# Value projection, first column pass: the fourth and the seventh chunk as seven block products

## The chip, the cores and the metric

The kernel runs on one core of a Trainium2 chip. The metric is the device time of one execution in microseconds (us), the median of three runs: 1117.72 us, from 1116.6 to 1118.2. A profile of one execution stands beside it.

## The reference, cut to what matters

The reference is one decoder layer on 256 tokens of width 2048, in float32: a combined projection, two groups of eight attention heads, an output projection, a layer norm, a gated feed-forward block with a short convolution, and a second layer norm. The change touches only the value columns of the first projection:

```python
proj = h @ w_in[l]            # h: 256 x 2048
v_d = proj[..., o0:o0 + DIFF_W]   # 8 heads x 128 columns
v_m = proj[..., o0:o0 + MOBA_W]   # 8 heads x 128 columns
```

Together that is a product of a 256 x 2048 matrix with a 2048 x 2048 matrix.

## The kernel before, in words

**Precision.** Each float32 operand is split into two fp32r parts, hi (a rounded copy, written by ScalarE, ACT) and lo (the rest, a subtraction by VectorE, DVE). A product of two operands is three matmuls: hi by hi, hi by lo, lo by hi. In the value projection the activations (tile x2, read as xh and xl) are the stationary side and 512 weight columns the moving side.

**Tiling.** The value projection runs in two column passes of 1024 columns. A pass goes over the 2048 rows of the weights in eight chunks of 256. Chunks are numbered 0 to 15 in the order of the list `stream`: 0 to 7 are the first pass, 8 to 15 the second. The fourth and the seventh chunk of the first pass are chunks 3 and 6. The four sums of a pass, two token halves by two column halves, stay in PSUM banks 0 to 3 (CB). A plain chunk is 2 x 2 x 2 blocks, eight products of three matmuls each: 24 matmuls of 128x512 (`mm_pair`).

**Seven products.** In chunks 9, 12 and 15 the eight products are replaced by seven (Winograd's form): the weights and the activations of a chunk are first combined into block sums, and of the seven products four (numbers 1, 5, 6 and 7) are shared by several of the four results. They gather in banks 4 to 7 (MB) and are added up once, at the end of the pass (`v_shared`). That is 21 matmuls (`mm_seven`), issued in the order 5, 7, 6, 4, 1, 2, 3. Products 5, 7, 6 and 4 read weight sums in the slots 3, 4, 5 and 6 of the tiles vhi and vlo, and products 1, 2 and 3 read the plain weight blocks in the slots 0 to 2. The lo part of slots 0 to 2 isn't made by DVE: ACT writes the negated hi part, and a DMA issued on POOL adds the raw weights to it (L626 and L627). vhi and vlo have one buffer each, so a second such chunk can't be prepared before TensorE is done with the one before it.

**Order of work.** Nothing is scheduled by a planner: each engine runs its instructions in the order in which the code is written. `begin(i)` comes before chunk i and prepares chunk i + 2, `middle(i)` stands in it, and a list of due steps (`at`, `pending`, `urgent`) adds what has to be done at a given chunk. For a chunk of seven products `begin(i)` calls `blocks_raw` and `act_sums` for chunk i + 2, `middle(i)` calls `blocks_lo`, `blocks_sum`, `act_sums_split`, `blocks_hi` and the split of chunk i + 3, and `begin(i + 1)` finishes slot 6. The engines ACT and DVE run ahead of TensorE as far as their inputs and their buffers allow. Raw weights come through the queue of SP into four slots in turn (raw0 to raw3), so chunk 7 reuses the slot of chunk 3, and chunk 10 that of chunk 6.

The lines the text speaks of: L177 and L179 make hi and lo of a plain chunk, L228 and L229 hi and lo of the activations, L626 to L633 are `blocks_raw`, L638, L655 and L661 the lo, the sum and the hi of the slots 3 to 6, L586 to L589 and L604 and L605 the sums of the activations and their split, L861 the copy of a finished bank, L855 and L858 `v_shared`, and L277 every matmul.

Of the kernel before, what the change touches and what calls it, by code (L numbers as in the profile page):

```python
# [11 lines left out]
F32 = mybir.dt.float32  # L12
F32R = mybir.dt.float32r
AF = mybir.ActivationFunctionType
ALU = mybir.AluOpType

P = 128
# [25 lines left out]
PT = FT // 2  # L43
VP = KT // 2


SEVEN = {"v": ((), range(1, 8, 3)), "d": (range(PT - 2), range(3, 16, 3))}

LATE = 2

# [7 lines left out]
def hymba_layer(ctx: ExitStack, tc: tile.TileContext, a: dict):  # L58
    nc = tc.nc
    PE, DVE, ACT, POOL, SP = nc.tensor, nc.vector, nc.scalar, nc.gpsimd, nc.sync  # L60

    def pool(name, bufs=1, space=None):
        kw = {} if space is None else {"space": space}
        return ctx.enter_context(tc.tile_pool(name=name, bufs=bufs, **kw))
# [3 lines left out]
    work = pool("work", 2)  # L68
# [157 lines left out]
    def split_x(k0, k1):  # L226
        t = xraw[:, k0 * S:k1 * S].rearrange("p (k t) -> p k t", t=S)
        ACT.activation(xh[:, k0:k1], t, AF.Copy)  # L228
        DVE.tensor_tensor(xl[:, k0:k1], t, xh[:, k0:k1].bitcast(F32), ALU.subtract)  # L229
# [83 lines left out]
    vals = keep.tile([P, 4, 2, 512], F32, name="val", tag="big")  # L313
# [5 lines left out]
    def at(step, fn, *args, rank=LATER):  # L319
        after.setdefault(step, []).append((rank, len(after.get(step, ())), fn, args))  # L320
# [205 lines left out]
    def down_slot():  # L526

        if "slot" not in kept:
            kept["slot"] = keep.tile([P, 16, 512], F32R, name="slot", tag="t2")
        return kept["slot"]  # L530
# [22 lines left out]
    aparts, sums = {}, {}  # L553
    sevens = [p for kind, p, n, j in stream if (kind, n) == ("d", 1) and j in SEVEN["d"][1]]

    def seven(i):
        kind, p, n, j = stream[i]
        return kind in SEVEN and (j if kind == "d" else p) in SEVEN[kind][n] and (kind, n) != ("d", 0)

# [52 lines left out]
    def blocks_raw(i):  # L612

        kind, p, n, _ = stream[i]
        t = loaded[i].rearrange("p (b c) -> p b c", c=512)
        if kind == "d":
            slot = down_slot()
            hi, lo = slot[:, 0:7], slot[:, 7:14]
        else:
            lo = keep.tile([P, 7, 512], F32R, name="vlo", tag="ma")  # L620
            hi = keep.tile([P, 7, 512], F32R, name="vhi", tag="mb")
        b11, _, b22, b12 = ORDER[kind]
        f = [work.tile([P, 512], F32, name="tf", tag="m1") for _ in range(2)]
        blocks[i] = (hi, lo, f)
        if kind == "v":
            ACT.activation(lo[:, 0:3], t[:, 0:3], AF.Copy, scale=-1.0)  # L626
            POOL.dma_start(lo[:, 0:3], t[:, 0:3], accum_op=ALU.add)  # L627
        DVE.tensor_tensor(f[0], t[:, b11], t[:, b12], ALU.subtract)
        DVE.tensor_tensor(f[1], t[:, b12], t[:, b22], ALU.add)
        for j in range(2):  # L630
            ACT.activation(hi[:, 3 + j], f[j], AF.Copy)
        if kind == "v":
            ACT.activation(hi[:, 0:3], t[:, 0:3], AF.Copy)  # L633
# [31 lines left out]
    MB = {1: bank[4], 5: bank[5], 6: bank[6], 7: bank[7]}  # L665
# [22 lines left out]
    def mm_pair(i, c, k):  # L688

        kind, _, n, _ = stream[i]  # L690
        ah, al = aparts[i, k]
        w = weights(i, 1024 * c + 512 * k, 512)
        for lhs, j in ((ah, 0), (al, 0), (ah, 1)):
            for t in range(2):
                mm_count((kind, n, t, c), CB[t][c], lhs[:, t * P:(t + 1) * P], w[j])

    def mm_seven(i, then={}):
        kind, _, n, _ = stream[i]
        hi, lo, _ = blocks.pop(i)
        s3, s1, s2, s4 = sums.pop(i)  # L700
        (h0, l0), (h1, l1) = (aparts[i, k] for k in ((0, 1) if kind == "d" else (1, 0)))
        a11, a12, a22 = (h0[:, 0:P], l0[:, 0:P]), (h1[:, 0:P], l1[:, 0:P]), (h1[:, P:], l1[:, P:])
        b11, b21, b22, _ = ORDER[kind]
        for m, lhs, b in ((5, s1, 3), (7, s3, 4), (6, s2, 5), (4, a22, 6), (1, a11, b11), (2, a12, b21), (3, s4, b22)):
            t, c = {2: (0, 0), 3: (0, 1), 4: (1, 0)}.get(m, (None, None))
            key, dst = ((kind, n, m), MB[m]) if t is None else ((kind, n, t, c), CB[t][c])
            if m == 4:
                middle(i)
            mm_three(key, dst, lhs, (hi[:, b], lo[:, b]))
            if m in then:  # L710
                then[m]()
# [62 lines left out]
    for kind, pairs in (("v", VP), ("d", PT)):  # L774
        for n in range(2):
            np_ = pairs - (PAIRED_END if kind == "d" and n == 1 else 0)
            n7 = len(SEVEN[kind][n])
            for m in MB:
# [20 lines left out]
    def begin(i):  # L799

        urgent(i)
        j = i + 2
        if j < NS and seven(j):
            blocks_raw(j)
            act_sums(j)
        elif j - 1 < NS and seven(j - 1):
            blocks_sum(j - 1, 1)
            split(j, 1)
            blocks_hi(j - 1, 1)
            blocks_lo(j - 1, 3)  # L810
            blocks_whole(j - 1)
        else:
            split(j, 0)
            split(j, 1)
        if i >= first_d:
            act_back(i + 3)
        load(i + 6)
        pending(i)

    def middle(i):  # L820

        urgent(i + 0.5)
        if i + 2 < NS and seven(i + 2):
            blocks_lo(i + 2, 0)
            blocks_sum(i + 2, 0)
            blocks_lo(i + 2, 1)
            act_sums_split(i + 2)
            blocks_hi(i + 2, 0)
            split(i + 3, 0)
            blocks_lo(i + 2, 2)  # L830
        elif i + 3 < NS and not seven(i + 3):
            split(i + 3, 0)
        pending(i + 0.5)
# [10 lines left out]
    def done(i):  # L844
        for half in range(2):
            parts.pop((i, half))

    def value(n, t, c):
        return vals[:, 2 * n + c, t]

    def v_shared(n):
# [4 lines left out]
        for t, c, m in ((0, 1, 5), (1, 1, 5), (0, 0, 0), (None, None, 6), (0, 1, 0), (None, None, 7), (1, 0, 0), (1, 1, 0)):  # L856
            dst = u if t is None else v[t, c]
            DVE.tensor_tensor(dst, dst, MB[m] if m else u, ALU.add)  # L858

    def v_copy(n, t, c):  # L860
        ACT.activation(value(n, t, c), CB[t][c], AF.Copy)  # L861

    def run_v(i):
        _, p, n, _ = stream[i]
        for k in range(2):
            aparts[i, k] = xh[:, 2 * p + k], xl[:, 2 * p + k]
        if i == first_q - 1:
            v_copy(1, 1, 1)
            mm_seven(i, {m: lambda tc=tc: v_copy(1, *tc) for m, tc in ((2, (0, 0)), (3, (0, 1)), (4, (1, 0)))})
            at(i + 1, v_shared, 1)  # L870
        elif seven(i):
            mm_seven(i)
        elif i < 2:
            for k in range(2):
                if k == 1:
                    middle(i)
                for c in range(2):
                    mm_pair(i, c, k)
            done(i)
        else:  # L880
            for c in range(2):
                if c == 1:
                    if i == VP - 1:
                        for t in range(2):
                            v_copy(0, t, 0)
                    middle(i)
                for k in range(2):
                    mm_pair(i, c, k)
            done(i)
        if i == VP - 1:  # L890
            for t in range(2):
                at(i + 1, v_copy, 0, t, 1, rank=0)
        for k in range(2):
            aparts.pop((i, k))

# [27 lines left out]
    for i in range(first_o):  # L923
        begin(i)
        if i < first_q:
            run_v(i)
        else:
            run_a(i)
        if i == 8:
            load_consts()  # L930
        if i == 11:
            lambdas()
        if i == 14:
            SP.dma_start(z, a["x"])
        if i == 14:
            load_table("cos_m")
            load_table("sin_m")
# [17 lines left out]
    for i in range(first_o, last[0]):  # L955
# [11 lines left out]
        if first_o + 8 <= i < first_o + 12:  # L967
            n = i - first_o - 8
# [326 lines left out]
    for i in range(first_d, NS - PAIRED_END):  # L1295
        begin(i)
        _, p, n, j = stream[i]
# [203 lines left out]
```

## Time and profile before

| | |
|---|---|
| median of 3 runs | 1117.72 us |
| lowest and highest run | 1116.6 and 1118.2 us |
| span of the profiled execution, first to last instruction | 1115.1 us |
| what the median has beyond that span | 2.6 us |
| PE busy in the span | 1105.6 us (99%) |
| DVE and ACT busy | 853.6 us (77%) and 682.1 us (61%) |
| first pass of the value projection on PE | from 4.69 to 49.67 us |

Of the profiled execution only the span is known, so its own time is taken as the span and 2.6 us around it. PE is TensorE's matmuls. In rows of the timeline the first number is the start in us from the beginning of the span, the second the us from the start of the first to the end of the last instruction in the row, then the engine, the line, the operation with its tiles and shapes, how many there are, and in brackets how long the engine had been idle and what ended that.

### The profile page before, as it was taken

The numbers are of one execution on the slowest core, as the hardware profiler recorded it, in microseconds if no ns is written. First come the engines' busy times: TensorE is split into PE (matmuls) and PEld (weight loads), VectorE is DVE, ScalarE is ACT, GpSimd is POOL, SyncE is SP. The second block draws the span as 40 slices with busy tenths as digits, with TensorE's granted clock in tenths as the row PEclk, the third lists the DMA queues.
The fourth block names the chain that finished last, engine by engine and source line by source line (L and its number), as shares of the span: only waits on it lengthen the run. The fifth ranks groups of instructions, "written<-read, shape, count | busy, mean of one in ns | idle before, by whom it ended". The sixth has DMA issues, their size and how long they took to land.

```text
span 1115.1 us, 15769 instructions
## 1 busy us (share of the span) xinstructions
PE 1105.6 (99%) x5929; PEld 952.2 (85%) x5929; DVE 853.6 (77%) x1400; ACT 682.1 (61%) x1077; POOL 57.4 (5%) x81
## 2 busy tenths in 40 slices
PE   9999999999999999999999999999999999999997
PEld 6888888888888898888888888888888888888886
DVE  6676778887745778878888887777777777678866
ACT  6655776644443486666666666666666666645552
POOL 0000110000000000000000000000000000001103
PEclk9999999999999999999999999999999999999999
DMA  9898866444455537977877877777777777688992
GB/s 330 281 285 288 258 199 199 165 152 157 174 198 189 189 116 260 295 255 246 268 258 258 267 247 250 255 238 259 248 247 249 244 245 252 199 320 296 324 323 77
DMA packets 59868, 266.46 MB, mean 239 GB/s; under 512 B 6080, under 2 KB 7568, under 8 KB 42000
## 3 DMA queue, kind: packets, MB, share of 16 engines
q1 hardware_dynamic: 51584, 229.81, 57.1%
q0 software_dynamic: 8064, 35.39, 14.2%
q8 instruction: 46, 0.75, 0.3%
q10 hardware_dynamic: 144, 0.26, 0.1%
q14 instruction: 30, 0.25, 0.1%
HBM read 227.93 MB, written 15.20 MB: 218 GB/s over the span
## 4 chain that ended last, share of the span: by engine, by line
PE 98%; DVE 1%; DMA 0%; ACT 0%; issue 0%; SPq 0%; DVEq 0%
PE bank L277 97%; PE bank L404 0%; DMA raw<-in_w_v 0%; PE bank L987 0%; PE bank L451 0%; ACT hf L990 0%; DVE h L1002 0%; DVE st L475 0%; DVE z L472 0%; DVE z L1349 0%; DVE z L1345 0%; DVEq L1497 0%; DVE mv L481 0%; ACT hi L208 0%; DVE h L1001 0%
## 5 line engine op out<-in xcount | busy, mean ns | idle before, releaser
L277 PE MATMUL bank<-h,hi 128*128 128x512 f32 x1376 | 480.9, 390 | 0.0
L277 PE MATMUL bank<-h,lo 128*128 128x256 f32 x1376 | 387.9, 282 | 0.0
L277 PEld LDWEIGHTS bank<-h,hi 128*128 128x128 f32 x1376 | 258.2, 188 | 54.5
L277 PEld LDWEIGHTS bank<-h,lo 128*128 128x128 f32 x1376 | 260.0, 189 | 3.7
L179 DVE TENSOR_TENSOR lo<-raw,hi 128x1024 fp32r<-128x1024 f32 x147 | 177.1, 1221 | 92.3 <-ACT hi L177 91.6
L196 DVE TENSOR_TENSOR lo<-raw,hi 128x1024 fp32r<-128x1024 f32 x171 | 206.8, 1220 | 25.1 <-ACT hi L188 24.9
L177 ACT ACTIVATE hi<-raw 128x1024 fp32r<-128x1024 f32 x155 | 161.5, 1055 | 86.4 <-PE bank L277 55.9
L277 PE MATMUL bank<-x,hi 128*128 128x512 f32 x512 | 183.4, 399 | 0.0
L188 ACT ACTIVATE hi<-raw 128x1024 fp32r<-128x1024 f32 x171 | 177.3, 1050 | 0.0
L277 PE MATMUL bank<-x,lo 128*128 128x256 f32 x512 | 144.3, 282 | 0.0
L1107 ACT ACTIVATE ub<-bank 128x512 f32<-128x512 f32 x86 | 51.4, 598 | 108.2 <-PE bank L277 105.2
L277 PEld LDWEIGHTS bank<-x,hi 128*128 128x128 f32 x512 | 96.2, 188 | 21.9 <-issue 2.7
L277 PEld LDWEIGHTS bank<-x,lo 128*128 128x128 f32 x512 | 96.8, 189 | 0.2
L1116 DVE TENSOR_TENSOR ub<-ub 128x256 f32<-128x256 f32 x86 | 36.4, 423 | 56.9 <-ACT ub L1107 56.9
L742 ACT ACTIVATE tslot<-tf 128x512 fp32r<-128x512 f32 x80 | 50.3, 628 | 43.5 <-DVE tf L1197 24.7
L745 DVE TENSOR_TENSOR tslot<-tf,tslot 128x512 fp32r<-128x512 f32 x80 | 55.2, 690 | 12.4 <-ACT tslot L742 10.3
L277 PE MATMUL bank<-hi,back 128*128 128x512 f32 (+1 forms) x216 | 58.9, 381 | 0.0
L277 PE MATMUL bank<-hi,x 128*128 128x512 f32 x208 | 56.0, 391 | 0.8 <-ACT hi L208 0.8
L277 PE MATMUL bank<-tslot,sp 128*128 128x512 f32 x180 | 47.8, 392 | 0.0
L277 PEld LDWEIGHTS bank<-hi,x 128*128 128x128 f32 x208 | 38.8, 188 | 9.9 <-ACT hi L208 2.0
L277 PEld LDWEIGHTS bank<-hi,back 128*128 128x128 f32 x216 | 40.2, 188 | 7.8
L277 PE MATMUL bank<-hi,mh 128*128 128x512 f32 x128 | 41.2, 394 | 0.0
(233 smaller groups left out, 1460.6 us busy)
## 6 DMA issues: line engine op xcount, KB each, us to landing
raw<-in_w_u SPq DMA_DIRECT2D x88, 1024.0 KB, 6.2
raw<-in_w_d SPq DMA_DIRECT2D x68, 512.0 KB, 6.8
raw<-in_w_qk SPq DMA_DIRECT2D x32, 1024.0 KB, 4.9
raw<-in_w_o SPq DMA_DIRECT2D x16, 1024.0 KB, 4.8
raw<-in_w_v SPq DMA_DIRECT2D x28, 512.0 KB, 7.6
ring<-in_w_d SPq DMA_DIRECT2D x20, 512.0 KB, 7.1
dparts<-rslot SPq DMA_DIRECT2D x20, 512.0 KB, 2.8
back<-dparts POOLq DMA_DIRECT2D x19, 512.0 KB, 7.2
```

Source lines behind the costliest of these rows:

```text
L177: ACT.activation(hi[:, s], t[:, x:y], AF.Copy)
L179: DVE.tensor_tensor(lo[:, s], t[:, x:y], hi[:, s].bitcast(F32), ALU.subtract)
L188: ACT.activation(hi, t[:, half * 1024:half * 1024 + 1024], AF.Copy)
L196: DVE.tensor_tensor(lo, t[:, half * 1024:half * 1024 + 1024], hi.bitcast(F32), ALU.subtract)
L277: PE.matmul(out, lhsT, rhs, start=start, stop=stop)
L742: ACT.activation(side["t"][:, 0, j], f, AF.Copy)
L745: DVE.tensor_tensor(side["t"][:, 1, j], f, side["t"][:, 0, j].bitcast(F32), ALU.subtract)
L1107: ACT.activation(t.rearrange("p j t -> p (j t)"), up_bank(i), AF.Copy)
L1116: DVE.tensor_tensor(u[:, 0], u[:, 0], u[:, 1], ALU.add)
```

## The change

The table SEVEN gets chunks 3 and 6 of the first pass. The block sums for them are made in the same way, at the same places of `begin` and `middle`; `blocks_raw` also splits the activations of its chunk, which the plain split did before. The shared products of chunks 3 and 6 are added up by `v_products` in the middle of chunk 7, into the part of the tile `vals` that belongs to the second pass and is still empty, and `v_sum` adds that part to the first pass's values in the middle of chunk 9.

```diff
-SEVEN = {"v": ((), range(1, 8, 3)), "d": (range(PT - 2), range(3, 16, 3))}
+SEVEN = {"v": (range(3, 8, 3), range(1, 8, 3)), "d": (range(PT - 2), range(3, 16, 3))}
...
             hi = keep.tile([P, 7, 512], F32R, name="vhi", tag="mb")
+        if kind == "v" and n == 0:
+            split_x(2 * p, 2 * p + 2)
...
+    def v_products():
+
+        w = {(t, c): value(1, t, c) for t in range(2) for c in range(2)}
+        u = work.tile([P, 512], F32, name="tf", tag="m1")
+        ACT.activation(w[0, 0], MB[1], AF.Copy)
+        for t, c, m, src in ((None, None, 6, w[0, 0]), (0, 1, 5, u), (1, 0, 7, u), (1, 1, 5, w[1, 0])):
+            DVE.tensor_tensor(u if t is None else w[t, c], MB[m], src, ALU.add)
+
+    def v_sum():
+        DVE.tensor_tensor(vals[:, 0:2], vals[:, 0:2], vals[:, 2:4], ALU.add)
...
+    at(VP - 0.5, v_products)
...
             for t in range(2):
                 at(i + 1, v_copy, 0, t, 1, rank=0)
+            at(i + 2.5, v_sum)
```

In the changed kernel the lines behind the first new ones have moved by two, and those behind the new functions by more: L628 in it is L626 here, L640 is L638, L874 is L861.

On ACT, from the preparation of chunk 3 (first row) to that of chunk 5 (last row), before (x is the activations, z their raw form):

```order
L228 ACTIVATE x_79<-z 128x2x256
L177 ACTIVATE hi<-raw 128x1024 x2
L228 ACTIVATE x_79<-z 128x2x256
L177 ACTIVATE hi<-raw 128x1024 x2
L228 ACTIVATE x_79<-z 128x2x256
L177 ACTIVATE hi<-raw 128x1024 x2
```

and in the changed kernel:

```order
L228 ACTIVATE x_79<-z 128x2x256
L628 ACTIVATE vlo<-raw 128x1536
L633 ACTIVATE vhi<-tf 128x512 x2
L635 ACTIVATE vhi<-raw 128x1536
L604 ACTIVATE vh<-vf 128x256
L604 ACTIVATE wh<-vf 128x256
L663 ACTIVATE vhi<-tf 128x512
L228 ACTIVATE x_79<-z 128x2x256
L177 ACTIVATE hi<-raw 128x1024 x2
L663 ACTIVATE vhi<-tf 128x512
L228 ACTIVATE x_79<-z 128x2x256
L177 ACTIVATE hi<-raw 128x1024 x2
```

Two copies of half a chunk have become eight instructions, and the two copies of chunk 4 and its activations now stand ahead of the last of them. On DVE the same stretch of the changed kernel, chunk 3 from the lo part of slot 3 to that of slot 6, is this:

```order
L640 TENSOR_TENSOR vlo<-tf,vhi 128x512
L657 TENSOR_TENSOR tf<-raw,tf 128x512
L640 TENSOR_TENSOR vlo<-tf,vhi 128x512
L605 TENSOR_TENSOR vl<-vf,vh 128x256
L605 TENSOR_TENSOR wl<-vf,wh 128x256
L229 TENSOR_TENSOR x_79<-z,x_79 128x2x256
L179 TENSOR_TENSOR lo<-raw,hi 128x1024
L640 TENSOR_TENSOR vlo<-tf,vhi 128x512
L657 TENSOR_TENSOR tf<-raw,tf 128x512
L179 TENSOR_TENSOR lo<-raw,hi 128x1024
L640 TENSOR_TENSOR vlo<-tf,vhi 128x512
```

Where two subtractions of half a chunk stood (L179 twice), slots 3 to 6 of vlo are now made one after the other, with the activations and both halves of chunk 4 between them. The third place is the turn of the passes on DVE, in the changed kernel, from slot 5 of chunk 9 to the first weight sum of chunk 12:

```order
L640 TENSOR_TENSOR vlo<-tf,vhi 128x512
L868 TENSOR_TENSOR tf<-bank_77,val 128x512
L868 TENSOR_TENSOR val<-bank_76,tf 128x512
L868 TENSOR_TENSOR val<-bank_78,tf 128x512
L868 TENSOR_TENSOR val<-bank_76,val 128x512
L657 TENSOR_TENSOR tf<-raw,tf 128x512
L179 TENSOR_TENSOR lo<-raw,hi 128x1024
L640 TENSOR_TENSOR vlo<-tf,vhi 128x512
L179 TENSOR_TENSOR lo<-raw,hi 128x1024 x2
L871 TENSOR_TENSOR val<-val 128x2048
L630 TENSOR_TENSOR tf<-raw 128x512
```

The four L868 (`v_products`) stand between slot 5 and slot 6 of chunk 9, and L871 (`v_sum`) ahead of the sums of chunk 12; bank_76, bank_77 and bank_78 are the banks 5, 6 and 7 of MB.

## The prediction

> **What bounds the kernel now.** The page first: the share of busy time and the chain that ended last.
>
> ```profile
> PE 1105.6 (99%) x5929; PEld 952.2 (85%) x5929; DVE 853.6 (77%) x1400; ACT 682.1 (61%) x1077; POOL 57.4 (5%) x81
> PE 98%; DVE 1%; DMA 0%; ACT 0%; issue 0%; SPq 0%; DVEq 0%
> ```
>
> The chain runs through TensorE for 98% of the span. The waits of PE over the whole span say how much slack it has; its three longest are these.
>
> ```profile
> PE bank L277 <- DVE idle L788: 1.2, 1, 1.2
> PE bank L277 <- ACT hi L208: 0.8, 1, 0.8
> PE bank L277 <- DVE h L1002: 0.7, 1, 0.7
> ```
>
> Nothing that comes late early on is made up for later: a matmul saved in the value projection shortens the span by its spacing, and a microsecond in which PE stands there lengthens it by as much. The timeline of PE has the first row of chunks 1, 3, 4, 9 and 10.
>
> ```profile
> 11.59 1.07 PE L277 MATMUL bank<-hi,x 128*128 128x512 f32 x4
> 22.47 1.07 PE L277 MATMUL bank<-hi,x 128*128 128x512 f32 x4
> 27.91 1.07 PE L277 MATMUL bank<-hi,x 128*128 128x512 f32 x4
> 55.11 0.39 PE L277 MATMUL bank<-vhi,vh 128*128 128x512 f32 x1
> 59.87 1.07 PE L277 MATMUL bank<-hi,x 128*128 128x512 f32 x4
> ```
>
> A plain chunk takes 27.91 - 22.47 = 5.44 us, 24 matmuls at 0.227 us. Chunk 9, of seven products, takes 59.87 - 55.11 = 4.76 us, 21 at the same spacing. So the saving is 3 x 0.227 = 0.68 us a chunk, 1.36 us for two, if each is ready in time. That is 0.12%, below the 0.2% which a measurement of this kernel can tell from no change. All else can only cost.
>
> **Chunk 3: when its weights are there.** Next I read when the inputs of chunk 3 arrive. ACT's timeline has its second half (19.51), then the activations and both halves of chunk 4; DVE splits activations too; the last row is the windows view, with granted clock, DMA share and GB/s at its end.
>
> ```profile
> 19.51 1.06 ACT L177 ACTIVATE hi<-raw 128x1024 fp32r<-128x1024 f32 x1 [0.22 <-PE bank L277]
> 20.47 0.61 ACT L228 ACTIVATE x<-z 128x512 fp32r<-128x512 f32 x1
> 21.46 1.06 ACT L177 ACTIVATE hi<-raw 128x1024 fp32r<-128x1024 f32 x1 [0.37 <-DMA raw<-in_w_v]
> 22.73 1.06 ACT L177 ACTIVATE hi<-raw 128x1024 fp32r<-128x1024 f32 x1 [0.21 <-PE bank L277]
> 21.75 0.68 DVE L229 TENSOR_TENSOR x<-z,x 128x512 fp32r<-128x512 f32 x1
> 20.00:30.00 10.00, 10.00 (x46) 8.29 (x45) 9.34 (x10) 8.11 (x10) 0.00 (x0) 1.00 1.03 405
> ```
>
> The row at 19.51 names PE, but the buffer it writes was chunk 0's, and PE had left chunk 0 by 11.59; so it waited for its weights, which land at about 19.5. The DMA engines are full here (share 1.03, 405 GB/s), so they can't land sooner. In the plain form that is enough: PE begins chunk 3 at 22.47, and each half needs one copy and one subtraction. The block sums of the seven products need both halves at once, so their whole preparation starts at 19.5, 3.0 us ahead of PE.
>
> How long it takes is read from chunk 12, prepared by the same instructions: ACT, then DVE, then POOL, then the landing of all L627 transfers, then of the L176 ones (512 KB each).
>
> ```profile
> 59.84 1.49 ACT L626 ACTIVATE vlo<-raw 128x1536 fp32r<-128x1536 f32 x1 [4.60 <-PE bank L277]
> 61.24 1.13 ACT L631 ACTIVATE vhi<-tf 128x512 fp32r<-128x512 f32 x2
> 63.65 0.40 ACT L604 ACTIVATE vh<-vf 128x256 fp32r<-128x256 f32 x1
> 64.26 0.62 ACT L661 ACTIVATE vhi<-tf 128x512 fp32r<-128x512 f32 x1
> 68.45 0.64 ACT L661 ACTIVATE vhi<-tf 128x512 fp32r<-128x512 f32 x1 [1.67 <-DVE tf L655]
> 56.60 0.68 DVE L628 TENSOR_TENSOR tf<-raw 128x512 f32<-128x512 f32 x1
> 67.00 0.68 DVE L638 TENSOR_TENSOR vlo<-tf,vhi 128x512 fp32r<-128x512 f32 x1
> 67.72 0.69 DVE L655 TENSOR_TENSOR tf<-raw,tf 128x512 f32<-128x512 f32 x1
> 68.33 1.22 DVE L179 TENSOR_TENSOR lo<-raw,hi 128x1024 fp32r<-128x1024 f32 x1
> 69.47 0.68 DVE L638 TENSOR_TENSOR vlo<-tf,vhi 128x512 fp32r<-128x512 f32 x1
> 61.65 0.92 POOL L627 DMA_DIRECT2D vlo<-raw  x1 [18.65 <-DMA vec<-in_vecs]
> DMA to landing us min/median/max: 8.6/8.6/9.8
> DMA to landing us min/median/max: 8.3/9.4/12.2
> ```
>
> From its first ACT row (59.84), vh is there after 4.2 us, slot 5 of vlo after 7.8 us, slot 6 after 70.15 - 59.84 = 10.3 us. Chunk 12 has that time: it starts once PE is done with chunk 9 (59.87), and PE plays chunks 10 and 11 meanwhile, 10.9 us. Chunk 3 has 3.0 us. To the times after vh I add 0.7 us for the activations of chunk 4, which now stand in between (0.61 on ACT, 0.68 on DVE). On chunk 12 the first weight sums (56.60) were done ahead; on chunk 3 they run beside L626, which takes as long as the two of them (1.49 against 2 x 0.68), so they add little. On the span's clock: vh 23.7, slot 5 at 19.5 + 7.8 + 0.7 = 28.0, slot 6 at 30.5.
>
> PE then: products 5 and 7 from 23.7 to 25.1; product 6 issues one matmul, stands until 28.0, ends at 28.5; product 4 waits for the hi part of slot 6 (about 29.3) and then for its lo part, 30.5, and ends at 31.0. Products 1, 2 and 3 need slots 0 to 2 of vlo, made by the accumulating DMA. It is issued 61.65 - 59.84 = 1.8 us after L626 starts, at 21.3, and lands 8.6 to 9.8 us later by its own kind, 29.9 to 31.1; by the longest L176, 12.2 us, at 33.5. Loads of chunks 4 to 6 fill the engines all that time, so I take 11.0, between the slowest of both kinds: 32.3. One matmul of product 1 goes ahead, eight follow, 8 x 0.227 = 1.8: chunk 3 ends at 34.1 in place of 27.91, **6.2 us late**. With the DMA out of the way it ends at 31.0 + 9 x 0.227 = 33.0 (5.1 late), with 12.2 at 35.3 (7.4 late); a transfer slowed still more, to 14 us, makes 9.2.
>
> The Trainium skill ("DMA: Bandwidth & Descriptors", the fit for a transfer issued by GpSimd) gives 2.0 us and the bytes by 436 GB/s. By it 768 KB would land after an estimated 3.8 us, never be waited for, and chunk 3 be 5.1 late rather than 6.2. The trace differs with 8.6 to 9.8 us for this transfer, so the measurement decides.
>
> **Chunk 6** saves its 0.68 us. Its buffers come free when chunk 3 ends, and PE plays chunks 4 and 5 meanwhile: 10.88 us, and 2.3 more until slot 6 is needed, 13.2 against 11.0. With that cover gone it would cost what chunk 3 costs. The weights of chunk 7 are a step moved: SP's queue may not refill chunk 3's slot before the accumulating DMA has read it. Such a wait is in the trace of SP's queue, with all later loads behind it; the second row is the loads of value weights, at the end their us to landing:
>
> ```profile
> SPq L151 <- DMA vlo<-raw: 9.4, 1, 9.4
> raw<-in_w_v SPq DMA_DIRECT2D x28, 512.0 KB, 7.6
> ```
>
> Chunk 7 is issued at 32.3, lands about 7.6 us later, at 40, is split in some 2 us and is due on PE at 34.1 + 2 x 5.44 + 4.76 = 49.7. It is hidden by chunks 4 to 6, with 7 us to spare; chunk 10, held up in the same way by chunk 6 until about 47, lands at 55 and is due at 66.
>
> **The turn of the passes.** Before, chunk 9 could be prepared early, its buffers being free. Now it starts when PE leaves chunk 6, call that 0, and PE wants chunk 9 at 10.88. The two bank copies on ACT stand ahead of vh, and the four new additions on DVE between slots 5 and 6; their nearest rows:
>
> ```profile
> 46.92 1.09 ACT L861 ACTIVATE val<-bank 128x512 f32<-128x512 f32 x2 [2.82 <-PE bank L277]
> 96.06 0.69 DVE L858 TENSOR_TENSOR tf<-tf,bank 128x512 f32<-128x512 f32 x1
> ```
>
> Slot 5 is done at 7.8 + 1.1 = 8.9, the additions at 8.9 + 4 x 0.69 = 11.7. Product 5 of chunk 9 overwrites the bank that the last of them reads, so PE waits until 11.7, 0.8 us. Slot 6 follows with a sum, half a plain chunk and its own subtraction at their spacings (67.72 to 68.33, 68.33 to 69.47, and 0.68): 14.1; PE wants it at 11.7 + 10 x 0.227 = 14.0, 0.2 us more. **1.0 us**; bounds 0, if the copies slip into ACT's gaps and DVE runs ahead, and 1.6, if the new copy of bank 4 (half of 1.09, 0.6) delays the additions too. I take the 1.0 of the rows. The sum over 2048 columns (`v_sum`) costs about 2 x 1.22 = 2.4 us of DVE ahead of chunk 12. Slot 6 of chunk 12 was ready at 70.15 and needed at 70.75 + 2.3 = 73.0, 2.9 us of slack, so it costs nothing, or up to 1 us if DVE is late from chunk 9.
>
> **The sum**: + 6.2 - 0.68 (chunk 6; chunk 3's saving is in the 6.2) + 1.0 = + 6.5. The span goes from 1115.1 to 1121.6, and the median, 2.6 us above it, to **1124.2 us**, 0.6% slower.
>
> **The rivals.**
>
> *The clock falls.* From 25.4 to 32.3 PE issues about seven matmuls, 1.6 us of 6.9. The end of the span shows what a gap does: the last matmul, then the granted clock in the windows behind it (third figure from the end: 1.00, 0.77, 0.50).
>
> ```profile
> 1108.45 0.73 PE L277 MATMUL bank<-rows,side 6*128 6x512 f32 x2 [0.36 <-ACT side L1417]
> 1109.00:1109.50 0.50, 0.18 (x1) 0.00 (x0) 0.50 (x2) 0.46 (x1) 0.00 (x0) 1.00 1.08 430
> 1109.50:1110.00 0.50, 0.00 (x0) 0.00 (x0) 0.50 (x2) 0.50 (x2) 0.00 (x0) 0.77 0.39 148
> 1110.00:1112.00 2.00, 0.00 (x0) 0.00 (x0) 0.33 (x1) 0.31 (x1) 0.00 (x0) 0.50 0.71 267
> ```
>
> It halves within a microsecond of the last matmul, after 2 us of thin work. Half a clock on the eight or nine matmuls behind the DMA costs about 2.0 us, as many again in chunk 4 up to 4; I take 2.4: 1126.6. Against it: no single gap here is over 2.7 us, and matmuls at full width stand between them. The Trainium skill ("TensorE: Matmul & The Clock Gate", Part 1) puts the fall behind a whole idle window of about 3.4 us; by that rule it would not come. The trace's end speaks for less.
>
> *Less is lost.* The DMA lands before 31 and the turn costs nothing: 5.1 - 0.7 = + 4.4, 1122.1.
>
> *A second late chunk.* Loads of chunks 7 to 9, all held back until 32, share the engines with the accumulating DMA of chunk 6, which lands at 34.1 + 1.8 + 12 = 48 and is due at 34.1 + 10.9 + 2.9 = 47.9; one of 14 us and a late turn add 3: 1127.2.
>
> *Not slower.* The preparation of chunk 3 is hidden, by weights that land early or by work that other engines overlap more than on chunk 12. It decides from the point where slot 6 is ready by 22.47 + 2.3 = 24.8, 5.3 us after landing in place of 11. Then only the saving is left: 1117.72 - 1.36 = 1116.4. The landing at full DMA and the rows of chunk 12 speak against it.
>
> **Chances.** The forecast 0.48 (its own range 1122.4 to 1126.2), the clock 0.25, less lost 0.11, a second late chunk 0.11, not slower 0.05. The range, 1121.2 to 1128.4, holds all but the last and the ends of the clock and of the late chunk. Slower by over 0.2% (above 1120.0) 0.95; within 0.2% 0.04, as the last rival's 1.36 us can't be told; faster 0.01.
>
> **What would show it.** PE's waits should name DVE vlo L640 (two of them, about 2.7 and 1 us) and the DMA vlo<-raw (about 1 us) near 25 to 32 us; chunk 3's first matmul should start near 23.7 and chunk 4's near 34; chunk 9 should wait for DVE L868 for under 1 us; the span should be 1121.6. The clock rival shows as a PEclk below 1.00 between 28 and 38. The prediction is wrong if PE reaches chunk 4 before 31, or if a wait over 2 us stands after chunk 4.

## The result and the profile after

| | before | changed |
|---|---|---|
| median | 1117.12 us (5 runs, 1116.6 to 1118.2) | 1124.08 us (5 runs, 1123.64 to 1125.67) |
| ratio, 95% interval | | 1.006, 1.0049 to 1.007 |
| span of the profiled execution | 1115.1 us | 1122.5 us |
| start of chunk 12 on PE | 70.75 us | 77.71 us |

The change costs 7.0 us, 0.6%, at a forecast of 1124.2 us. In the profiled execution 77.71 - 70.75 = 6.96 us are lost by chunk 12, and the rest of the program adds 0.4 us. Two of all the executions below were far longer than the rest of their kernel, one of the kernel before (1372 us) and one of the kernel with chunk 6 and the additions split (3937 us), and are left out of medians and ratios.

The page of the changed kernel, its busy shares and its chain: PE's share of the chain falls from 98% to 88%, and those of the DMA, DVE and ACT grow.

```profile
PE 1110.2 (99%) x5923; PEld 952.4 (85%) x5923; DVE 867.0 (77%) x1429; ACT 688.6 (61%) x1090; POOL 59.6 (5%) x83
PE 88%; DMA 5%; DVE 3%; ACT 2%; issue 1%; SPq 0%; DVEq 0%; ACTq 0%
```

PE has six matmuls fewer (5923 against 5929) and yet is busy 4.6 us longer (1110.2 against 1105.6): some of them took longer than before. PE's waits for instructions of the changed parts (L640, L663 and L604 make slots and splits of the block sums, L868 is the new additions of `v_products`):

```profile
PE bank L277 <- DVE vlo L640: 2.5, 2, 2.3
...
PE bank L277 <- ACT vh L604: 0.5, 1, 0.5
...
PE bank L277 <- DVE val L868: 0.3, 1, 0.3
PE bank L277 <- ACT vhi L663: 0.2, 1, 0.2
```

Together these waits are 3.5 us. Half of the loss shows as no wait of PE at all. PE's timeline has where the rest is: chunk 3 (22.97 to 34.39), chunk 6 (45.29 to 50.37), chunk 9's start (61.86) and chunk 12 (77.71).

```profile
22.97 0.50 PE L277 MATMUL bank<-vhi,vh 128*128 128x512 f32 x1 [0.53 <-ACT vh L604]
...
24.48 0.40 PE L277 MATMUL bank<-vhi,wh 128*128 128x512 f32 x1
27.14 0.80 PE L277 MATMUL bank<-vlo,wh 128*128 128x512 f32 x1 [2.26 <-DVE vlo L640]
...
29.60 0.79 PE L277 MATMUL bank<-vlo,x 128*128 128x512 f32 x1 [0.28 <-DVE vlo L640]
...
31.30 0.79 PE L277 MATMUL bank<-vlo,x 128*128 128x512 f32 x1
...
34.39 1.08 PE L277 MATMUL bank<-hi,x 128*128 128x512 f32 x4
...
61.86 0.50 PE L277 MATMUL bank<-vhi,vh 128*128 128x512 f32 x1 [0.26 <-DVE val L868]
...
77.71 0.39 PE L277 MATMUL bank<-vhi,vh 128*128 128x512 f32 x1
```

Between 24.48 and 27.14 PE issues nothing: it stands for slot 5. The matmul at 27.14 takes 0.8 us, where the one at 22.97, also behind a wait, took 0.5. The windows view says why, in the third figure from the end, the granted clock:

```profile
24.00:26.00 2.00, 0.87 (x4) 0.38 (x2) 1.44 (x2) 2.00 (x3) 0.00 (x0) 1.00 1.08 321
26.00:28.00 2.00, 0.86 (x2) 0.50 (x2) 1.97 (x4) 0.33 (x2) 0.00 (x0) 0.74 1.06 268
28.00:30.00 2.00, 1.55 (x3) 0.69 (x3) 2.00 (x3) 2.00 (x4) 0.00 (x0) 0.50 1.00 268
30.00:32.00 2.00, 1.94 (x5) 1.03 (x5) 2.00 (x3) 1.41 (x2) 0.00 (x0) 0.50 0.76 297
32.00:34.00 2.00, 2.00 (x7) 1.57 (x6) 2.00 (x4) 0.00 (x0) 0.00 (x0) 0.55 0.76 261
34.00:36.00 2.00, 2.00 (x11) 1.61 (x9) 1.21 (x5) 1.65 (x2) 0.00 (x0) 1.00 0.95 324
```

From about 27.0 to 33.8 TensorE runs at half its clock (0.74 in the window from 26 is half a clock for its last 1.04 us, 0.55 in that from 32 a full one for its last 0.2). Seven matmuls in 32 to 34 keep it wholly busy, where ten did before. That is why the lost time is counted as busy time. The clock is back at 1.00 when chunk 4 begins.

The steps of the preparation of chunk 3, from ACT's, DVE's, POOL's and SP's timelines, and the landing of the accumulating DMA:

```profile
18.71 1.49 ACT L628 ACTIVATE vlo<-raw 128x1536 fp32r<-128x1536 f32 x1 [1.71 <-DMA raw<-in_w_v]
26.39 0.69 DVE L640 TENSOR_TENSOR vlo<-tf,vhi 128x512 fp32r<-128x512 f32 x1
28.86 0.69 DVE L640 TENSOR_TENSOR vlo<-tf,vhi 128x512 fp32r<-128x512 f32 x1
20.52 1.05 POOL L629 DMA_DIRECT2D vlo<-raw  x1 [20.07 <-ACT vlo L628]
31.40 2.99 SPq L151 DMA_DIRECT2D raw<-in_w_v  x6
DMA to landing us min/median/max: 10.7/10.9/12.2
```

The weights land at 18.7, slot 5 is ready at 27.1, slot 6 at 29.55, and the transfer issued at 20.52 lands some 10.7 us later, at about 31.25. PE's first matmul of product 1 that needs it starts at 31.30, and SP's held-back loads leave at 31.40.

### The profile page after: what moved, and what is told of

It is laid out like the page before. It is cut to its first block, busy times and chain, and to the rows that moved or that the text cites. A ratio compares the mean times of both kernels' runs of the same rounds, so it can differ in the third digit from the quotient of the medians.

```text
span 1122.5 us, 15804 instructions
## 1 busy us (share of the span) xinstructions
PE 1110.2 (99%) x5923; PEld 952.4 (85%) x5923; DVE 867.0 (77%) x1429; ACT 688.6 (61%) x1090; POOL 59.6 (5%) x83
## 4 chain that ended last, share of the span: by engine, by line
PE 88%; DMA 5%; DVE 3%; ACT 2%; issue 1%; SPq 0%; DVEq 0%; ACTq 0%
PE bank L277 87%; DMA raw<-in_w_d 3%; DMA vlo<-raw 1%; DVE slot L648 1%; DMA raw<-in_w_v 1%; ACT slot L647 1%; ACT hi L177 1%; DMA z<-in_xT 0%; PE bank L404 0%; DVE z L1265 0%; DVE tf L657 0%; DVE slot L640 0%; DVE lo L179 0%; SPq L139 0%; PE bank L1003 0%
## 5 line engine op out<-in xcount | busy, mean ns | idle before, releaser
L179 DVE TENSOR_TENSOR lo<-raw,hi 128x1024 fp32r<-128x1024 f32 x143 | 172.0, 1221 | 87.6 <-ACT hi L177 87.6
L196 DVE TENSOR_TENSOR lo<-raw,hi 128x1024 fp32r<-128x1024 f32 x171 | 206.9, 1221 | 25.1 <-ACT hi L188 24.9
L177 ACT ACTIVATE hi<-raw 128x1024 fp32r<-128x1024 f32 x151 | 156.7, 1054 | 80.8 <-PE bank L277 51.7
L188 ACT ACTIVATE hi<-raw 128x1024 fp32r<-128x1024 f32 x171 | 177.3, 1050 | 0.0
L747 DVE TENSOR_TENSOR tslot<-tf,tslot 128x512 fp32r<-128x512 f32 x80 | 55.3, 691 | 12.4 <-ACT tslot L744 10.3
L277 PE MATMUL bank<-hi,x 128*128 128x512 f32 x176 | 48.1, 395 | 0.0
L277 PE MATMUL bank<-hi,ml 128*128 128x512 f32 x128 | 40.8, 389 | 0.0
## 6 DMA issues: line engine op xcount, KB each, us to landing
raw<-in_w_v SPq DMA_DIRECT2D x28, 512.0 KB, 10.8
```

The lines of the kernel that those rows point to most:

```text
L177: ACT.activation(hi[:, s], t[:, x:y], AF.Copy)
L179: DVE.tensor_tensor(lo[:, s], t[:, x:y], hi[:, s].bitcast(F32), ALU.subtract)
L188: ACT.activation(hi, t[:, half * 1024:half * 1024 + 1024], AF.Copy)
L196: DVE.tensor_tensor(lo, t[:, half * 1024:half * 1024 + 1024], hi.bitcast(F32), ALU.subtract)
L277: PE.matmul(out, lhsT, rhs, start=start, stop=stop)
L747: DVE.tensor_tensor(side["t"][:, 1, j], f, side["t"][:, 0, j].bitcast(F32), ALU.subtract)
```

## How the experiments are read

Runs of one of these kernels differ among each other by 1 us and sometimes by 4 (the kernel with chunk 5 alone, below: 1117.57 to 1121.46). Part of that goes with the clock: the record has the mean granted clock of each execution, and with chunk 4 alone, below, the five executions at 0.998 took 1119.5 to 1120.7 us, the four at 0.996 and 0.997 took 1121.0 to 1123.0. Part arises far behind the change: in the profiled execution without the accumulating DMA a group of matmuls near the second down pass, at 1077.66, waits 0.23 us for DVE, where no work of the value projection is near.

So effects below some 2 us are read from PE's timeline, of one profiled execution for each kernel. Chunk 1's first row is taken as the origin (11.59 before, 11.40 in the changed kernel), which takes out a program that merely starts earlier. **Late at chunk 4** is the distance from there to chunk 4's first row, less the 27.91 - 11.59 = 16.32 of the kernel before; **late at chunk 12** is the same with 70.75 - 11.59 = 59.16. For the changed kernel they are 34.39 - 11.40 - 16.32 = 6.67 us and 77.71 - 11.40 - 59.16 = 7.15 us. This origin suits a chunk at which PE doesn't wait. A chunk 3 that waits ends when its operands are there, whenever PE began chunk 1; so kernels that wait there are compared by the start of chunk 4 itself. Three kernels below do the same work up to chunk 4 (changed, chunk 3 alone, additions split): their 6.63 to 7.21 shows how far single executions differ. All runs, with the rows that these are from:

| kernel | chunk 1 | chunk 4 | chunk 12 | late at 4 | late at 12 | median | ratio, 95% interval |
|---|---|---|---|---|---|---|---|
| changed | 11.40 | 34.39 | 77.71 | 6.67 | 7.15 | 1124.08 | 1.006 (1.0049 to 1.007) |
| chunk 3 alone | 11.81 | 35.34 | 78.59 | 7.21 | 7.62 | 1124.75 | 1.0066 (1.0051 to 1.0081) |
| chunk 4 alone | 11.65 | | 73.67 | | 2.86 | 1120.68 | 1.0032 (1.0022 to 1.0042) |
| chunk 5 alone | 11.46 | | 71.98 | | 1.36 | 1118.89 | 1.0017 (1.0007 to 1.0026) |
| chunk 6 alone | 12.02 | | 71.33 | | 0.15 | 1117.37 | 0.9999 (0.9989 to 1.0008) |
| PE kept busy | 11.71 | 33.23 | 77.03 | 5.20 | 6.16 | 1124.25 | 1.0064 (1.0047 to 1.0081) |
| no DMA at chunk 3 | 11.04 | 33.57 | 76.57 | 6.21 | 6.37 | 1124.85 | 1.007 (1.0055 to 1.0085) |
| both | 11.30 | 32.79 | 75.75 | 5.17 | 5.29 | 1123.80 | 1.0058 (1.0043 to 1.0073) |
| additions split | 11.35 | 34.30 | 76.48 | 6.63 | 5.97 | 1125.29 | 1.0069 (1.0054 to 1.0084) |
| chunk 3 reordered | 11.67 | 30.14 | 74.68 | 2.15 | 3.85 | 1121.59 | 1.0034 (1.0022 to 1.0045) |
| chunk 6, additions split | 11.39 | | 69.88 | | -0.67 | 1116.68 | 0.9996 (0.9987 to 1.0005) |

The first four experiments ran on the same chip with a median before of 1117.17 us, the next four with 1116.98, the last two with 1117.39.

## Experiment: the same form at one chunk alone

The theory: weights land too late for PE at chunk 3, and each later chunk has 2.2 us more, since a load stream runs ahead of PE by that much a chunk. The rival: the turn and the additions set the loss, whichever chunk it is. Chunk 3, 4, 5 or 6 alone takes the new form, with the same additions at the turn:

```diff
-SEVEN = {"v": (range(3, 8, 3), range(1, 8, 3)), ...
+SEVEN = {"v": ((3,), range(1, 8, 3)), ...          (and (4,), (5,), (6,))
```

> Seven products in chunk 3 alone. Theory (chunk 3's inputs land too late for its preparation): the profile after has the accumulating DMA 6.0 us later than product 1 wants it, less the 0.68 saved, and 1.3 us for the clock: chunk 4 starts on TensorE 6.7 us later than before, the turn costs nothing since the buffers are free early; 6.7 us slower in all, chunk 9 without a wait. Rival (the work at the turn of the passes sets the loss): half of the loss or less is gone with chunk 6, under 4 us slower.

> Seven products in chunk 4 alone. Theory: weights land 3.25 us later per chunk, TensorE comes 5.44 us later per chunk, so each chunk further on has 2.2 us more: the DMA comes 3.8 us late instead of 6.0, 3.1 us slower, and up to 1.3 more if the clock falls. Rival (turn): the same loss as with chunk 3 alone.

> Seven products in chunk 5 alone. Theory: the DMA comes 1.6 us late, less 0.68: 0.9 us slower, clock at 1.00. Rival (turn): the same loss as with chunk 3 alone.

> Seven products in chunk 6 alone. Theory: chunk 6 is ready in time and saves 0.7 us, the turn costs the 0.8 us that it costs in the changed kernel: within 0.5 us of the kernel before, with a wait on the additions of the shared sums ahead of chunk 9. Rival (turn): several us slower.

The medians went up by 7.6, 3.5, 1.7 and 0.2 us, and chunk 12 was late by 7.6, 2.9, 1.4 and 0.15 us. The turn is in all four; it can't set the loss. With chunk 4 alone PE's waits in the chunk are for slots 5 and 6, as in chunk 3, with the first shorter by a microsecond (2.26 to 1.23), and the clock stays up in the profiled execution. PE's timeline, then the windows view with the clock third from the end:

```profile
30.95 0.50 PE L277 MATMUL bank<-vlo,wh 128*128 128x512 f32 x1 [1.23 <-DVE vlo L640]
...
32.34 0.49 PE L277 MATMUL bank<-vhi,x 128*128 128x512 f32 x1 [0.66 <-ACT vhi L663]
33.41 0.50 PE L277 MATMUL bank<-vlo,x 128*128 128x512 f32 x1 [0.58 <-DVE vlo L640]
```

The windows:

```profile
30.00:32.00 2.00, 0.73 (x2) 0.30 (x2) 1.97 (x4) 0.35 (x1) 0.00 (x0) 1.00 1.05 255
32.00:34.00 2.00, 1.08 (x4) 0.67 (x4) 2.00 (x4) 1.75 (x3) 0.00 (x0) 1.00 0.92 266
```

With chunk 5 alone the wait for slot 5 is gone, and the waits for the hi and the lo of slot 6 remain, in PE's timeline:

```profile
36.24 0.50 PE L277 MATMUL bank<-vhi,x 128*128 128x512 f32 x1 [0.66 <-ACT vhi L663]
37.31 0.50 PE L277 MATMUL bank<-vlo,x 128*128 128x512 f32 x1 [0.58 <-DVE vlo L640]
```

With chunk 6 alone no matmul of the chunk waits: it takes 43.98 - 39.22 = 4.76 us, exactly the 21 matmuls, and saves 0.68; the turn then takes that back, and 0.15 us more by chunk 12. The first rows of chunks 6 and 7:

```profile
39.22 0.39 PE L277 MATMUL bank<-vhi,vh 128*128 128x512 f32 x1
...
43.98 1.07 PE L277 MATMUL bank<-hi,x 128*128 128x512 f32 x4
```

So chunk 6 is the first at which the form pays, and what it pays the additions cost. The sizes at chunks 4 and 5 came near what was expected (2.9 and 1.4 us at chunk 12, where 3.1 and 0.9 were), but not for the reason given: the accumulating DMA was to come 3.8 and 1.6 us late, and PE's waits there name the block sums and not the DMA. Chunk 3 alone cost 0.9 us more than the 6.7 expected.

## Experiment: the clock and the accumulating DMA, apart and together

In chunk 3 of the changed kernel two things come late near each other: the clock falls, and the transfer lands. Both were taken away, each alone and then together. To keep the clock up, PE multiplies zeros into a free bank in its waits (19 matmuls that no result uses):

```diff
+        fill = {(6, 0, 1): 10, (4, 0, 0): 3, (4, 0, 1): 3, (1, 0, 0): 3} if i == 3 else {}
...
-            mm_three(key, dst, lhs, (hi[:, b], lo[:, b]))
+            for x, y in ((0, 0), (0, 1), (1, 0)):
+                for _ in range(fill.get((m, x, y), 0)):
+                    mm(MB[1], idle[:, 0:P], idle, True, True)
+                mm_count(key, dst, lhs[x], (hi[:, b], lo[:, b])[y])
```

> The changed kernel with 19 matmuls on zeros put into TensorE's waits in chunk 3 (bank 4, not yet in use), so that it isn't idle. Theory (the half clock costs 1.3 us of its own): the granted clock stays at 1.00, products 1, 2 and 3 run at 0.227 us spacing behind the DMA, chunk 4 starts 1.3 us earlier than in the changed kernel, 5.7 us slower than before. Rival (the clock falls in time that is lost anyway): no change, 7.0 us slower.

The clock stayed at 1.00 throughout (two windows below, then PE's timeline). One matmul of product 1 waited for the DMA, at the same time as in the changed kernel (31.30), and from there the matmuls followed at 0.227 us; chunk 4 starts at 33.23 in place of 34.39, 1.16 us earlier, where 1.3 was expected.

```profile
26.00:28.00 2.00, 1.91 (x9) 0.71 (x7) 1.97 (x4) 0.33 (x2) 0.00 (x0) 1.00 1.11 269
28.00:30.00 2.00, 2.00 (x8) 0.69 (x6) 2.00 (x4) 2.00 (x4) 0.00 (x0) 1.00 0.94 253
```

PE's timeline at chunk 3, chunk 4 and chunk 6:

```profile
31.30 0.51 PE L277 MATMUL bank<-vlo,x 128*128 128x512 f32 x1 [0.21 <-DMA vlo<-raw]
...
33.23 1.07 PE L277 MATMUL bank<-hi,x 128*128 128x512 f32 x4
...
47.75 0.50 PE L277 MATMUL bank<-vlo,x 128*128 128x512 f32 x1 [0.54 <-DMA vlo<-raw]
```

The last of these rows is chunk 6, where PE, now earlier, waits 0.54 us for the second accumulating DMA: of the 1.16 us won at chunk 4, 0.68 are left at chunk 12 (77.03 against 77.71). The median doesn't show them: it is 7.3 us above its own before, nearer to the rival's 7.0 than to the 5.7 expected, although the mean clock was 0.998 or 0.999 in all four executions.

Without the accumulating DMA in chunk 3 (the lo of its three plain weight blocks keeps only the negated hi part, so the time is that of a kernel which leaves the raw weights out of it):

```diff
-            POOL.dma_start(lo[:, 0:3], t[:, 0:3], accum_op=ALU.add)
+            if i != 3:
+                POOL.dma_start(lo[:, 0:3], t[:, 0:3], accum_op=ALU.add)
```

> The changed kernel without the accumulating DMA of chunk 3 alone (the lo part of its three plain weight blocks is left wrong, so the values are). Theory: with the clock at half, TensorE reaches product 1 only 0.3 us before the DMA lands, so 0.3 us is won: 6.7 us slower than before. Rival (the DMA is the last thing that chunk 3 waits for and sets the loss): 1 us or more is won.

Chunk 4 starts at 33.57, 0.82 us earlier than with the DMA, between the 0.3 expected and the rival's 1; the median, 7.9 us above its before, shows no gain. The clock fell all the same, only later, at about 29.2, and was back at about 32.7. It was down half as long as in the changed kernel, so part of the 0.82 is the clock's. The windows view:

```profile
26.00:28.00 2.00, 0.73 (x2) 0.30 (x2) 1.97 (x4) 0.33 (x2) 0.00 (x0) 1.00 0.79 302
28.00:30.00 2.00, 1.00 (x2) 0.69 (x3) 2.00 (x4) 2.00 (x4) 0.00 (x0) 0.81 0.64 210
30.00:32.00 2.00, 2.00 (x6) 1.53 (x5) 2.00 (x3) 1.29 (x2) 0.00 (x0) 0.50 0.96 307
32.00:34.00 2.00, 2.00 (x8) 1.59 (x8) 2.00 (x4) 0.45 (x1) 0.00 (x0) 0.84 0.97 377
```

Both edits together:

> Both: zeros in the waits and no accumulating DMA for chunk 3 (wrong lo part of its plain blocks). Theory: the two hide each other, and together they win more than each: chunk 3 ends 2.0 us behind slot 6, at 32.1 instead of 34.4, so 2.3 us is won, 4.7 us slower than before, all of it the block sums on ACT and DVE. Rival (clock or DMA alone): the same as the better one of the two.

Chunk 4 starts at 32.79, 1.60 us earlier than in the changed kernel, where 2.3 was expected. Three zero matmuls ahead of product 1, which had nothing to wait for any more, held it up by about 0.5 us (30.08 to 30.55), so without them chunk 4 would start at an estimated 32.3. PE's timeline:

```profile
30.08 0.82 PE L277 MATMUL bank<-idle 128*128 128x512 bf16 x3
30.55 0.58 PE L277 MATMUL bank<-vhi,x 128*128 128x512 f32 x1
...
32.79 0.84 PE L277 MATMUL bank<-hi,x 128*128 128x512 f32 x3
```

What follows. In these three kernels and the changed one the weights of chunk 3 are there at nearly the same time (L628 starts between 18.59 and 18.71), and product 4 reads the lo of slot 6 between 29.47 and 29.60; so their starts of chunk 4 can be set against each other.

- **The block sums.** With neither the DMA nor the fall of the clock chunk 4 starts at 32.3 to 32.8, still 4.4 to 4.9 us behind the 27.91 of the kernel before. That much of the 34.39 - 27.91 = 6.48 us is the block sums on ACT and DVE.
- **The clock** is worth 34.39 - 33.23 = 1.2 us with the DMA there, and without it 33.57 - 32.79 = 0.8, or some 1.3 without the zeros' 0.5.
- **The DMA** is worth 33.23 - 32.79 = 0.4 us with the clock up, or some 0.9 without the zeros' 0.5. With the clock down these runs don't separate it, as the clock was down for different lengths.

Each figure is from one execution of each kernel. The medians of the three are 6.8 to 7.9 us above their before, where 4.7 to 6.7 was expected, and lie within the spread of runs around the changed kernel's 1124.08; they confirm none of it.

## Experiment: the additions at the turn in two parts

The additions that read a bank stay ahead of slot 6 of chunk 9, two of them after ACT has copied banks 4 and 5; the two that read only SBUF go behind slot 6:

```diff
+        ACT.activation(w[1, 1], MB[5], AF.Copy)
+        DVE.tensor_tensor(u, MB[6], w[0, 0], ALU.add)
+        DVE.tensor_tensor(w[1, 0], MB[7], u, ALU.add)
...
+    def v_rest():
+        u, w = kept.pop("vp")
+        DVE.tensor_tensor(w[0, 1], u, w[1, 1], ALU.add)
+        DVE.tensor_tensor(w[1, 1], w[1, 1], w[1, 0], ALU.add)
...
-    at(VP - 0.5, v_products)
+    at(VP, v_products, rank=1)
+    at(VP, v_rest)
```

> The changed kernel with the additions at the turn in two parts: behind the copies of the finished banks ACT copies banks 4 and 5, DVE makes two additions from banks 6 and 7 ahead of slot 6 of chunk 9, and the two that read no bank stand behind slot 6. Theory: chunks 8 and 9 lose nothing, 0.8 us is won, 6.2 us slower than before, no wait on L868's successor ahead of chunk 9. Rival (DVE is late there anyway): under 0.3 us is won.

PE's timeline at the first row of chunk 9: the wait for L868 is gone, and so are 0.16 us by which a row of chunk 8 had been stretched.

```profile
60.84 0.39 PE L277 MATMUL bank<-vhi,vh 128*128 128x512 f32 x1
```

Chunk 12 is late by 5.97 us instead of 7.15. Of these 1.2 us the turn has 0.8 (chunks 7 to 9 take 15.64 us again, 49.96 to 65.60, against 16.46), and chunk 6, which takes 49.96 - 45.18 = 4.78 us here against 5.08, has 0.3. The median did not fall: it is 8.3 us above its before, where 6.2 was expected. The profiled execution, at a mean clock of 0.997, is the shortest with 1122.93 us; the other three, 1124.8 to 1125.9 us, had 0.994 and 0.995, so the clock was down for longer in them. The gain is seen in the trace alone.

## Experiment: chunk 3 first on DVE

If the preparation of chunk 3 is what is late, it must help to give it DVE and ACT before chunk 4's split, and to make the lo of the plain blocks with one subtraction on DVE in place of the ACT copy and the DMA:

```diff
+            if i + 2 == 3:
+                blocks_lo(3, 2)
+                t = loaded[3].rearrange("p (b c) -> p b c", c=512)
+                blocks_sum(3, 1)
+                blocks_hi(3, 1)
+                blocks_lo(3, 3)
+                DVE.tensor_tensor(blocks[3][1][:, 0:3], t[:, 0:3], blocks[3][0][:, 0:3].bitcast(F32), ALU.subtract)
```

with the same steps left out for chunk 3 at their old places.

> The changed kernel with chunk 3's block sums in another order: slots 5 and 6 directly behind slot 4 on ACT and DVE, the split of chunk 4 behind them, and the lo part of its three plain blocks by one subtraction on DVE in place of ACT's negated copy and the accumulating DMA. Theory: slot 6 is ready near 26.4 and the plain blocks near 28.1, 9.4 us behind the landing of the weights, chunk 4 starts near 29.9, 2.2 us later than before in place of 6.7; with chunk 6 and the turn as they are 2.6 us slower than before: the rest is that the weights land too late for any such preparation. Rival (DVE and ACT are full there, so what is moved only comes back at chunk 4): no earlier than 33.

The median is 1121.59 us, 4.2 above before, where 2.6 was expected and 7.0 is the changed kernel's loss. At chunk 4 it did what the theory says: slot 6 is ready at 26.46, PE reaches chunk 4 at 30.14, late by 2.15 us. But ACT and DVE, held up by chunk 3, prepare chunk 6 late. In PE's timeline the first row is chunk 4's start, and the other two are waits of chunk 6 that it has neither in the changed kernel nor alone:

```profile
30.14 1.07 PE L277 MATMUL bank<-hi,x 128*128 128x512 f32 x4
...
43.64 0.50 PE L277 MATMUL bank<-vhi,x 128*128 128x512 f32 x1 [0.42 <-ACT vhi L663]
44.72 0.49 PE L277 MATMUL bank<-vlo,x 128*128 128x512 f32 x1 [0.57 <-DVE vlo L640]
```

ACT's timeline shows ACT idle for 2.72 us, until DVE makes the first weight sum of chunk 6:

```profile
35.20 1.16 ACT L633 ACTIVATE vhi<-tf 128x512 fp32r<-128x512 f32 x2 [2.72 <-DVE tf L630]
```

Chunk 6 takes 47.36 - 41.02 = 6.34 us in place of 4.76, so 1.6 us come back, though at chunk 6 and not at chunk 4; late at chunk 12 is 3.85. Both theories were half right: the edit is worth 34.39 - 30.14 = 4.25 us at chunk 3, and ACT and DVE then have no room left for chunk 6. The order has only a part of the 4.25: the edit also leaves out the accumulating DMA, and the clock stays at 1.00, where no wait of chunk 3 is over 0.70 us. By the experiment before last these two together cost 1.6 to 2.1 us; no run changed the order alone.

## Experiment: chunk 6 alone, with the additions split

What is left if only the part that pays is kept.

```diff
-SEVEN = {"v": (range(3, 8, 3), range(1, 8, 3)), ...
+SEVEN = {"v": ((6,), range(1, 8, 3)), ...          (and the additions in two parts)
```

> Seven products in chunk 6 alone, with the additions at the turn in two parts. Theory: nothing waits, 0.7 us is won: chunk 12 starts 0.7 us earlier than before, 1116.4 against 1117.1, less than a comparison of medians can tell. Rival (the turn still costs): as with chunk 6 alone, no change.

No matmul of chunks 6 to 12 waits. Chunk 12 starts 0.67 us earlier than before against its origin, where 0.68 was the whole saving, and the span is 1114.4 us.

The ratio is 0.9996 (0.9987 to 1.0005). The trace shows the saving; the measurement can't tell it from no change.

## Why the prediction was right, and where not

The time was forecast at 1124.2 us and measured at 1124.08; the cause, the late operands of chunk 3, was the one named. Step by step:

- **PE bounds all, so a wait there is paid in full.** Held in the changed kernel: 6.96 us at chunk 12, 6.96 in the median. The other way round it is not shown: gains of 0.7 to 2.0 us at chunk 12 (77.03, 76.57, 75.75 and 76.48 against 77.71) left the medians where they were.
- **The saving of 0.68 us a chunk.** Held: chunk 6 alone takes 4.76 us, and with the additions split 0.67 us remain at chunk 12.
- **The preparation of chunk 3 as on chunk 12, 11.0 us from the landing to slot 6.** It took 29.55 - 18.71 = 10.84. The two waits for L640 came, of 2.3 us (2.7 forecast) and 0.3 (1 forecast; the rest had moved into the slow matmuls ahead of it).
- **The landing of the weights, taken as 19.5.** Right for the kernel before, where the second half was issued at 10.84 and landed at 19.4, as SP's line shows:

```profile
L151 SPq DMA_DIRECT2D raw<-in_w_v x1: 587/587/587, 10.8 to 10.8; - x1
DMA to landing us min/median/max: 8.6/8.6/8.6
```

In the changed kernel the same load was issued at 10.37 and landed 8.2 us later, so L628, which needs both halves, starts at 18.71. In the profiled executions with the new form at chunk 3 this load landed at 18.5 to 19.0, in those without at 19.2 to 19.7. Why is open.

- **The accumulating DMA, taken to land after 11.0 us, 32.3.** Its duration was right (10.7), and as it was issued 0.8 us earlier it landed at 31.25. It was to cost 1.1 us beyond the block sums; with the clock up the runs show 0.4 to an estimated 0.9. The wait of about 1 us that was to name it did not come, since PE, slowed by the clock, arrived at nearly the same time. The Trainium skill's fit ("DMA: Bandwidth & Descriptors"), by which this transfer would take an estimated 3.8 us, is far from the 10.7 to 12.2 us that these transfers took in the changed kernel.
- **The clock: forecast as unchanged, with 0.25 for a fall at 2.4 us.** This is the step that failed. The granted clock was 0.50 from 27.0 to 33.8. From the landing of the DMA (31.30) to chunk 4 PE took 3.09 us, where it took 1.93 with PE kept busy: 1.16 us more. The rival named the sign that came (a clock under 1.00 between 28 and 38). Its price of 2.4 was too high for this execution, in which the clock was back ahead of the last two matmuls of chunk 3, but not for every one: with chunk 3 alone, where it was down until 36.2, the same stretch took 3.58 us, and the first six matmuls of chunk 4 took 1.78 in place of 1.38. The argument against it, that no gap exceeds 2.7 us, doesn't hold: a gap of 2.3 us, with little work around it, was enough.
- **Chunk 6 saves 0.68.** In the changed kernel only 0.36 (it took 5.08 us): its DMA took 12.2 us from 36.16 and landed after PE wanted it.
- **The turn, 1.0 us.** 0.82, with the wait for L868 at 0.26 us (under 1, as forecast) and the rest in rows that were stretched.
- **Loads held back at SP, hidden.** Held: SP stood until 31.40, and no matmul of chunks 7 and 8 waited for its weights, though loads of value weights took a median of 10.8 us to land, where 7.6 was taken.
- **The 2.6 us between span and median.** Too much by 0.8. On record every execution is 1.7 to 1.8 us longer than its span (the profiled one 1124.29 against 1122.5); the 2.6 set the median of three executions against the span of another one. With 1.8 the forecast span of 1121.6 would have given 1123.4.

So the sum came out right by errors of both signs, and that it did so to 0.1 us is luck. At chunk 3 the operands came 1.0 us earlier than taken and the clock cost 1.2, so that chunk 4 starts at 34.39, where 34.1 was forecast. Chunk 6 lost 0.3 us of its saving, the turn cost 0.2 less, and 0.4 arose behind chunk 12; so the span is 0.9 us above the forecast 1121.6, and the 2.6 us, too large by 0.8, make up for that. With the weights at 18.7, a DMA of 10.7 us and a steady clock the same working gives chunk 4 at 31.25 + 1.8 = 33.1; with PE kept busy 33.23 was measured. Of the rivals, the second late chunk and the hidden preparation did not come.

## What to carry to other kernels

Matmuls saved in one place count only if their operands are ready there: take the time that the preparation needs from a place where it already runs (10.3 us plus what stands in between), and set it against the time from the landing of the raw data to the point at which TensorE arrives. Here that took the loss from 7.6 us at chunk 3 to 2.9, 1.4 and 0.15 at the next three, and another order of the work on ACT and DVE, together with one DMA left out, moved more (77.71 - 74.68 = 3.0 us at chunk 12) than the arithmetic saved (0.68 a chunk). And price a gap of TensorE twice: what it lasts, here 2.3 us, and what the matmuls behind it cost at half the clock, here 1.2.

## What the runs showed of the hardware that was not expected

**Behind a gap of 2.3 us, with little work around it, the clock halved for 3.4 or 6.8 us.** Of the kernels with chunk 3 in the new form, the four that left a gap of 2.3 us empty all lost the clock there: the changed kernel, chunk 3 alone, no DMA, and additions split. In all 17 of their executions the mean clock was 0.994 to 0.997, where it was 0.998 or 0.999 in 47 of 48 of the kernel before. Chunk 3 reordered and chunk 4 alone, with waits of at most 0.70 and 1.23 us, did not in the profiled execution. When it fell, and for how long, differed behind the same gap. The windows view with chunk 3 alone:

```profile
28.00:30.00 2.00, 0.77 (x3) 0.24 (x2) 2.00 (x4) 1.81 (x3) 0.00 (x0) 0.84 1.01 251
...
34.00:36.00 2.00, 2.00 (x6) 1.55 (x5) 2.00 (x3) 0.17 (x1) 0.00 (x0) 0.50 1.02 348
36.00:38.00 2.00, 2.00 (x9) 1.60 (x9) 0.24 (x1) 0.00 (x0) 0.00 (x0) 0.95 0.99 315
```

and with the additions split:

```profile
28.00:30.00 2.00, 0.77 (x3) 0.28 (x2) 2.00 (x4) 1.85 (x3) 0.00 (x0) 0.96 0.97 247
...
32.00:34.00 2.00, 2.00 (x7) 1.60 (x7) 2.00 (x4) 0.00 (x0) 0.00 (x0) 0.68 0.73 256
```

Worked out as above, the clock was down from 27.0 to 33.8 in the changed kernel and from 29.4 to 36.2 with chunk 3 alone, 6.8 us each, and from 29.2 to 32.7 without the DMA and from 29.8 to 33.3 with the additions split, 3.4 us each. The Trainium skill ("TensorE: Matmul & The Clock Gate", Part 1) says that the clock is set by a freely running window of about 3.4 us, and falls after one that is idle. The lengths and the varying moment agree with such a window. That it must be idle as a whole does not: no 3.4 us without a matmul occur in these chunks, and the longest wait was 2.3. In the 3.41 us ahead of the fall PE was busy for 1.2 to 1.3 us in all four. With chunk 4 alone a stretch as thin (1.23 us busy from 30.00 to 33.40) passed without a fall in the profiled execution, but four of its nine executions had a mean clock of 0.996 or 0.997 against 0.998 in the others, as a window at another place would make it. Where the clock fell in those is not on record, and three of ten executions with chunk 5 alone, whose profile has no such stretch, had such a mean too.

**Matmuls on zeros kept it at 1.00.** Nineteen of them in the same gaps were enough in both profiles, and in all eight executions of the two kernels the mean clock was 0.998 or 0.999.

**The accumulating DMA became slower.** 768 KB took a median of 8.6 us in the kernel before, 10.9 in the changed kernel and 11.0 with chunk 6 alone. Why is open: other loads are under way beside them, and no run changed those alone.
